# A hybrid attention, RWKV-7 and PEER block on one Trainium2 core: half of the low gate tables on ScalarE, and gate products with tokens innermost in PSUM

## The chip, the cores and the metric

The kernel runs on one core of a Trainium2 chip. The metric is the device time of one execution in microseconds (us), shown as a median over runs. The profile is one execution taken by the hardware profiler. TensorE (PE) does matmuls into PSUM, VectorE (DVE), ScalarE (ACT) and GpSimd (POOL) work on elements, and SyncE (SP) and ScalarE issue DMA transfers. TensorE has a clock of two levels, 1.2 and 2.4 GHz, of which the profile shows the granted share.

## The reference

For 512 tokens of width 1024 it computes a mixing part (sliding-window attention and an RWKV-7 recurrence, gated and projected) and a feed-forward part that picks experts by product keys (PEER). Only the second part matters here. For each token and each of 8 heads, 128 first and 128 second keys are scored; the best 16 pairs give 16 experts with softmax gates, 128 slots per token in all:

```python
s1, i1 = lax.top_k(sc[:, :, 0], PEER_TOPK)
s2, i2 = lax.top_k(sc[:, :, 1], PEER_TOPK)
...
top, pos = lax.top_k(cand, PEER_TOPK)
idx = jnp.take_along_axis(cidx, pos, axis=-1)
gate = jax.nn.softmax(top, axis=-1)
...
hpre = jnp.einsum('ckd,cd->ck', u_tab[ic], xc).astype(f32)
act = jax.nn.gelu(hpre, approximate=False) * gc
return jnp.einsum('ck,ckd->cd', act.astype(v_tab.dtype), v_tab[ic])
```

## The kernel before

For 384 of the 512 tokens the kernel doesn't gather experts; it computes all 16,384 of them densely, 128 experts (one second key, all first keys) at a time, and multiplies the activations with a dense gate that is zero where an expert wasn't picked. For the last 128 tokens the rows are gathered by indirect DMA.

The dense gate of a token is a 128 x 128 matrix over first and second keys. It is a product over the 128 slots: a one-hot table of the first key, times a one-hot table of the second key that carries the gate. To keep precision with f16 operands, the gate is scaled by GSC and split into a high part and a low part, and two products are added up in PSUM. Tokens come in 48 groups of 8. For group `i`, the function `onehots(i)` makes both one-hot tables in one VectorE comparison (L551, tile "ot", five buffers), `gated(i)` makes the high table (L557, tile "hi", four buffers) and, in place, the low table (L558, in "ot"), both on VectorE with the tokens of a pair innermost (GB2 = 2), and `gates(i)` does 16 matmuls of 128 x 128 x 128 (L571) into two PSUM tiles of 4 tokens and lets ScalarE bring each to SBUF (L574, "stg") with tokens innermost. After two groups a slice is kept on chip (L576, "gt0") and the 16 tokens' matrices go to DRAM by a DMA on ScalarE's queue (L577).

The stage around it is `window`. There the order of TensorE and of VectorE is the one written by hand: group `i` issues `onehots(i + 1)`, `gated(i)`, now and then a piece of the top-k code of a later block (PIECES), `gates(i - 2)` and 4 or 8 steps of the expert stage's first matmuls (`U`, from `u_stream`). ScalarE and POOL take the order that the framework's planner gives them. The steps of `u_stream` multiply the tokens with an expert block's weights: half of them in three f32r products of split operands (L96 to L98), half in plain f32 (L342, two instructions each). ScalarE makes the high part of these weights (L139) and POOL the low part (L140); ScalarE also applies the activation to the result (L352, out of two "mm" banks of PSUM). Twelve steps (RES) are kept back for the time after the last group, when the first gated activation is made (`v_first`: POOL L365, ScalarE L101, VectorE L102). PSUM tiles named "w" have six buffers.

`Topk.topk(b)` leaves, for each block of 128 tokens, the indices in `ids` and both parts of the gate in `gps`, in f16: the high part by ScalarE (L738), the low part by POOL (L739).

```python
for i in range(NG8):
    if i + 1 < NG8:
        onehots(i + 1)
    gated(i)
    go(PIECES.get(i, ()))
    if i >= LAG:
        gates(i - LAG)
    U(UN[i % len(UN)] + UX * (i in PIECES))
    go(POST.get(i, ()))
```

Of the kernel before, what the change touches and what calls it, by code (L numbers as in the profile page):

```python
# [10 lines left out]
F32 = mybir.dt.float32  # L11
# [5 lines left out]
AF = mybir.ActivationFunctionType  # L17
# [9 lines left out]
P = 128  # L27
# [5 lines left out]
NKEY = 128  # L33
# [18 lines left out]
NG8 = TD // 8  # L52
GSC = 2.0 ** 15
PLAIN = AHEAD - 2
GB2 = 2
# [481 lines left out]
def window(tc, ps, g_dram, u_stream, qst, tst, tk, tk0, scores, late_scores, gt0, v_first, whole):  # L537
    nc = tc.nc
    V, S, G, PE = nc.vector, nc.scalar, nc.gpsimd, nc.tensor
    ids, gps, row128 = tk.ids, tk.gps, tk.row128  # L540
    with ExitStack() as st:
        tk.sp = st.enter_context(tc.tile_pool(name="sp", bufs=1, reuse_waits="tile"))
        hot = {}
        stg = []

        def per_token(t):
            return t.rearrange("p (a b) -> p a b", b=GB2)[:, :, None, :].to_broadcast([P, t.shape[1] // GB2, NKEY, GB2])

        def onehots(i):
            hot[i] = ob.tile([P, 2, 8 // GB2, NKEY, GB2], F16, name="ot", bufs=OB + 1)  # L550
            V.tensor_tensor(hot[i].rearrange("p a q e t -> p (a q) e t"), per_token(ids[:, i]),  # L551
                            row128[:, None].to_broadcast([P, 16 // GB2, NKEY, GB2]), op=ALU.is_equal)

        def gated(i):
            ot = hot[i]
            hi = ob.tile([P, 8 // GB2, NKEY, GB2], F16, name="hi", bufs=OB)
            V.tensor_mul(hi, ot[:, 1], per_token(gps[:, i, 0:8]))  # L557
            V.tensor_mul(ot[:, 1], ot[:, 1], per_token(gps[:, i, 8:16]))  # L558
            hot[i] = ot[:, 0], (hi, ot[:, 1])

        def gates(i):
            o1, o2 = hot.pop(i)
            c, g8 = divmod(i, GCH // 8)
            if g8 == 0:
                stg[:] = [ob.tile([P, NKEY, GCH], F32, name="stg", bufs=2)]
            for q in range(2):
                pg = ps.tile([P, 4, NKEY], F32, name="w", bufs=6)
                for t in range(4):
                    for n in range(2):
                        qq, tt = divmod(q * 4 + t, GB2)  # L570
                        PE.matmul(pg[:, t], o1[:, qq, :, tt], o2[n][:, qq, :, tt], start=n == 0, stop=n == 1,  # L571
                                  skip_group_check=True)
                c0 = g8 * 8 + q * 4
                S.activation(stg[0][:, :, c0:c0 + 4].rearrange("p e t -> p t e"), pg, AF.Copy, scale=1.0 / GSC)  # L574
            if g8 == GCH // 8 - 1:
                S.activation(gt0[:, c], stg[0][:, :E2B], AF.Copy)  # L576
                nc.scalar.dma_start(g_dram[c], stg[0])  # L577

        us = u_stream()

        left = [AHEAD * KD - RES]

        def U(n):
            n = min(n, left[0])
            left[0] -= n
            for _ in range(n):
                next(us)

        with tc.manual_schedule(engines={mybir.EngineType.PE, mybir.EngineType.DVE}):
            tks = [tk0, *(tk.topk(b) for b in range(1, NB))]  # L590

            def go(todo):
                for b in todo:
                    next(tks[b], None)

            for h in range(HEADS):
                scores(1, h)
                go(SLOT[h])
            late_scores()
            whole()  # L600
            qst.close()
            ob = st.enter_context(tc.tile_pool(name="ob", bufs=2, reuse_waits="tile"))
            for n, todo in UN0:
                U(n)
                go(todo)
            onehots(0)
# [9 lines that stand above are left out]
            for i in range(NG8 - LAG, NG8):  # L616
                gates(i)
            v_first()
            for _ in us:
                pass  # L620
    tst.close()


class Topk:
    def __init__(self, tc, dump, ident, ps, tp, sc, idxU, idxV, ggate):
        self.tc, self.dump, self.ident, self.ps, self.tp, self.sc = tc, dump, ident, ps, tp, sc
        self.idxU, self.idxV, self.ggate = idxU, idxV, ggate
        V, G = tc.nc.vector, tc.nc.gpsimd
        self.sixteen = tp.tile([P, TOPK], U32, name="sixteen")
        V.memset(self.sixteen, 16)  # L630
        self.row16 = tp.tile([P, TOPK, TOPK], BF16, name="row16")
        self.row128 = tp.tile([P, NKEY, GB2], F16, name="row128")
        for t, w in ((self.row16, TOPK), (self.row128, GB2)):
            G.iota(t, pattern=[[1, t.shape[1]], [0, w]], base=0, channel_multiplier=0,
                   allow_small_or_imprecise_dtypes=True)
        self.ids = tp.tile([P, NG8, 16], F16, name="ids")
        self.gps = tp.tile([P, NG8, 16], F16, name="gps")

    def top16(self, jobs):
        V = self.tc.nc.vector  # L640
        for vals, idx, src in jobs:
            V.max(vals[:, 0:8], src)
        for vals, idx, src in jobs:
            V.max_index(idx[:, 0:8], vals[:, 0:8], src)
        for vals, idx, src in jobs:
            V.match_replace(src, vals[:, 0:8], src, FMIN)
        for vals, idx, src in jobs:
            V.max(vals[:, 8:16], src)
        for vals, idx, src in jobs:
            V.max_index(idx[:, 8:16], vals[:, 8:16], src)  # L650

    def topk(self, b):
        nc, ps, sc, ident, dump = self.tc.nc, self.ps, self.sc, self.ident, self.dump
        V, S, G, PE = nc.vector, nc.scalar, nc.gpsimd, nc.tensor
        ids, gps, tp = self.ids, self.gps, self.tp
# [18 lines left out]
        for r in range(4):  # L674
            na, w = 1 << r, TOPK >> r
# [51 lines left out]
        if b < ND:  # L727
            yield
            pt = ps.tile([P, 3, P], F32, name="w", bufs=6)
            for n, src in enumerate((i1, i2, gf)):  # L730
                PE.transpose(pt[:, n], src, ident)
            gr = slice(b * P // 8, (b + 1) * P // 8)
            g = sp.tile([P, HEADS, TOPK], F32, name="rg").rearrange("p h s -> p (h s)")
            g = g.rearrange("p (i t) -> p i t", t=8)
            for n, dst in enumerate((ids[:, gr, 0:8], ids[:, gr, 8:16], g)):
                S.activation(dst, pt[:, n].rearrange("p (i t) -> p i t", t=8), AF.Copy, scale=GSC if n == 2 else 1.0)
            hi, lo = gps[:, gr, 0:8], gps[:, gr, 8:16]
            S.activation(hi, g, AF.Copy)  # L738
            G.tensor_sub(lo, g, hi)  # L739
        else:  # L740
            V.scalar_tensor_tensor(self.idxU, i1, float(NKEY), i2, op0=ALU.mult, op1=ALU.add)
            V.scalar_tensor_tensor(self.idxV, i2, float(NKEY), i1, op0=ALU.mult, op1=ALU.add)
            V.tensor_copy(self.ggate, gf)
# [705 lines left out]
```

## Time and profile before

| what | value |
|---|---|
| time, median of 3 runs | 1825.45 us (1820.81 to 1827.6) |
| the profiled execution's own time | 1818.6 us |
| its span, first to last instruction | 1816.7 us |
| mean granted TensorE clock | 0.978 |
| stage of the gate tables | about 664 to 886 us |

In rows of the trace, times are microseconds unless marked ns. A group of instructions is written as line, engine, operation, output tile and input tiles, shapes and count, then busy time and mean ns of one, then the idle time of the engine just before them and what ended it. "PEld" is the weight load of TensorE. The end of a matmul is modelled; the pace of TensorE is read from start to start.

### The profile page before, as it was taken

The numbers are of one execution on the slowest core, as the hardware profiler recorded it, in microseconds if no ns is written. First come the engines' busy times: TensorE is split into PE (matmuls) and PEld (weight loads), VectorE is DVE, ScalarE is ACT, GpSimd is POOL, SyncE is SP. The second block draws the span as 40 slices with busy tenths as digits, with TensorE's granted clock in tenths as the row PEclk, the third lists the DMA queues.
The fourth block names the chain that finished last, engine by engine and source line by source line (L and its number), as shares of the span: only waits on it lengthen the run. The fifth ranks groups of instructions, "written<-read, shape, count | busy, mean of one in ns | idle before, by whom it ended". The sixth has DMA issues, their size and how long they took to land.

```text
span 1816.7 us, 30025 instructions
## 1 busy us (share of the span) xinstructions
PE 1714.3 (94%) x10933; PEld 1432.8 (79%) x10933; DVE 1349.0 (74%) x2564; ACT 720.4 (40%) x1415; POOL 780.5 (43%) x634
## 2 busy tenths in 40 slices
PE   7998899899999789898799999999999999998998
PEld 6765666667778668676689999999999999997886
DVE  4667665754535999999677777677788788788886
ACT  4553132221335436666633333333333333333334
POOL 5534232311155412122255555555455555556450
PEclk9998899999999889999899999999999999999999
DMA  6221111111564225563799999999989999998864
GB/s 210 81 64 41 36 42 48 36 48 54 184 205 133 88 76 178 199 216 142 243 320 325 305 313 325 317 303 317 321 302 318 322 302 320 327 309 290 297 222 167
DMA packets 193397, 378.98 MB, mean 209 GB/s; under 512 B 18624, under 2 KB 65472, under 8 KB 190176
## 3 DMA queue, kind: packets, MB, share of 16 engines
q1 hardware_dynamic: 97344, 175.71, 28.5%
q0 software_dynamic: 36864, 134.23, 22.1%
q10 hardware_dynamic: 59040, 67.12, 10.9%
q8 instruction: 86, 1.41, 0.3%
q14 instruction: 63, 0.52, 0.1%
HBM read 342.12 MB, written 33.55 MB: 207 GB/s over the span
## 4 chain that ended last, share of the span: by engine, by line
PE 45%; DVE 3%; issue 1%; DMA 1%; ACT 0%; POOL 0%; DVEq 0%; SPq 0%; POOLq 0%; ACTq 0%
PE w L96 8%; PE w L97 8%; PE w L98 8%; PE mm L96 7%; PE mm L98 7%; PE mm L97 7%; DMA vraw<-v_t 1%; DVE al L102 1%; DVE gacc L416 1%; DVE vl L102 0%; DVE wxl L102 0%; ACT w L467 0%; DVE gt L466 0%; DMA wraw<-v_t 0%; DVE wl L102 0%
## 5 line engine op out<-in xcount | busy, mean ns | idle before, releaser
L140 POOL TENSOR_TENSOR wl<-wraw,wh 128x512 fp32r<-128x512 f32 (+1 forms) x95 | 133.1, 1401 | 347.4 <-ACT wh L139 292.8
L96 PE MATMUL w<-vh,al 128*128 128x512 f32 x678 | 265.1, 391 | 6.8 <-DVE al L102 6.7
L97 PE MATMUL w<-vl,ah 128*128 128x512 f32 x678 | 264.6, 390 | 0.0
L98 PE MATMUL w<-vh,ah 128*128 128x512 f32 x678 | 264.4, 390 | 0.0
L399 POOL DMA_INDIRECT grow<-v_t,idxV x128 | 175.8, 1373 | 185.3 <-DVE gacc L416 152.1
L352 ACT ACTIVATE big<-mm 128x384 f32<-128x384 f32 x128 | 63.0, 492 | 464.6 <-PE mm L98 372.6
L399 POOL DMA_INDIRECT grow<-u_rows,idxU x128 | 167.9, 1312 | 183.4 <-DVE grow L406 164.3
L140 DVE TENSOR_TENSOR wl<-wraw,wh 128x512 fp32r<-128x512 f32 x101 | 103.8, 1028 | 153.2 <-ACT wh L139 128.4
L96 PE MATMUL mm<-x2h,wl 128*128 128x384 f32 (+1 forms) x576 | 199.2, 346 | 7.6 <-ACT big L352 6.2
L98 PE MATMUL mm<-x2h,wh 128*128 128x384 f32 (+1 forms) x576 | 191.7, 333 | 0.0
L97 PE MATMUL mm<-x2l,wh 128*128 128x384 f32 (+1 forms) x576 | 191.7, 333 | 0.0
L139 ACT ACTIVATE wh<-wraw 128x512 fp32r<-128x512 f32 (+1 forms) x196 | 122.4, 624 | 133.1 <-PE mm L763 53.0
L416 DVE SCALAR_TENSOR_TENSOR gacc<-grow,act,gacc 128x1024 f32<-128x1024 f32 x127 | 166.2, 1309 | 2.2
L102 DVE TENSOR_TENSOR vl<-vraw,vh 128x512 fp32r<-128x512 f32 x217 | 147.8, 708 | 25.5 <-ACT vh L101 25.1
L96 PEld LDWEIGHTS w<-vh,al 128*128 128x128 f32 x678 | 127.6, 188 | 33.3 <-DVE al L102 9.9
L365 POOL TENSOR_TENSOR big<-big,gt 128x384 f32<-128x384 f32 x128 | 135.8, 1064 | 34.3 <-ACT gt L576 21.2
L406 DVE SCALAR_TENSOR_TENSOR grow<-grow,xg 128x1024 f32<-128x1024 f32 x128 | 150.1, 1217 | 0.0
L98 PEld LDWEIGHTS w<-vh,ah 128*128 128x128 f32 x678 | 127.4, 188 | 26.8
L97 PEld LDWEIGHTS w<-vl,ah 128*128 128x128 f32 x678 | 127.5, 188 | 23.0
L96 PE MATMUL mm<-x2h,wxl 128*128 128x384 f32 (+1 forms) x436 | 143.5, 329 | 0.0
L97 PE MATMUL mm<-x2l,wxh 128*128 128x384 f32 (+1 forms) x436 | 143.4, 329 | 0.0
L98 PE MATMUL mm<-x2h,wxh 128*128 128x384 f32 (+1 forms) x436 | 143.4, 329 | 0.0
(388 smaller groups left out, 3944.0 us busy)
## 6 DMA issues: line engine op xcount, KB each, us to landing
wraw<-u_t SPq DMA_DIRECT2D x256, 256.0 KB
vraw<-v_t SPq DMA_DIRECT2D x217, 256.0 KB
g_dram<-stg ACTq DMA_DIRECT2D x24, 1024.0 KB
gt<-g_dram ACTq DMA_DIRECT2D x60, 384.0 KB
wraw<-wz SPq DMA_DIRECT2D x72, 256.0 KB
wraw<-v_t SPq DMA_DIRECT2D x39, 256.0 KB
wraw<-wq SPq DMA_DIRECT2D x32, 256.0 KB
wraw<-wproj SPq DMA_DIRECT2D x16, 256.0 KB
```

The lines of the kernel that those rows point to most:

```text
L96: PE.matmul(o, ll, rh, start=start, stop=False)
L97: PE.matmul(o, lh, rl, start=False, stop=False)
L98: PE.matmul(o, lh, rh, start=False, stop=stop)
L102: V.tensor_sub(lo, src, hi.bitcast(F32))
L139: S.activation(wh[:, :, :m], raw[:, :, :m], AF.Copy)
L140: lo.tensor_sub(wl[:, :, :m], raw[:, :, :m], wh[:, :, :m].bitcast(F32))
L352: S.activation(H[e], o, AF.Gelu)
L365: G.tensor_mul(ht, ht, g[:, :, e % E2B, :])
L399: G.indirect_dma_start(out=r, out_offset=None, in_=src, in_offset=bass.IndirectOffsetOnAxis(ap=idx[:, i:i + 1], axis=0))
L406: V.scalar_tensor_tensor(r, r, 1.0, xg, op0=ALU.mult, op1=ALU.mult, accum_out=hpre[:, s:s + 1])
L416: V.scalar_tensor_tensor(gacc, r, act[:, i:i + 1], gacc, op0=ALU.mult, op1=ALU.add)
```

## The change

In even groups the low table is made by ScalarE, with eight scaled copies, one for each token: each reads and writes in place the 128 elements of one token's table (every second f16 of a pair's rows) and takes that token's low gate from a new f32 tile, "gpl", as its per-partition scale. In odd groups VectorE makes it as before. "gpl" is written by one more POOL subtraction for each block. The gate products write PSUM with the four tokens innermost, so the 128 columns of a product lie 16 bytes apart, and the evacuation on ScalarE then reads PSUM in order and writes runs of four f32.

```diff
--- before.py
+++ after.py
@@ -555,7 +555,12 @@
             ot = hot[i]
             hi = ob.tile([P, 8 // GB2, NKEY, GB2], F16, name="hi", bufs=OB)
             V.tensor_mul(hi, ot[:, 1], per_token(gps[:, i, 0:8]))
-            V.tensor_mul(ot[:, 1], ot[:, 1], per_token(gps[:, i, 8:16]))
+            if i % 2:
+                V.tensor_mul(ot[:, 1], ot[:, 1], per_token(gps[:, i, 8:16]))
+            else:
+                for t in range(8):
+                    o = ot[:, 1, t // GB2, :, t % GB2]
+                    S.activation(o, o, AF.Copy, scale=tk.gpl[:, i, t:t + 1])
             hot[i] = ot[:, 0], (hi, ot[:, 1])
 
         def gates(i):
@@ -564,14 +569,14 @@
             if g8 == 0:
                 stg[:] = [ob.tile([P, NKEY, GCH], F32, name="stg", bufs=2)]
             for q in range(2):
-                pg = ps.tile([P, 4, NKEY], F32, name="w", bufs=6)
+                pg = ps.tile([P, NKEY, 4], F32, name="w", bufs=6)
                 for t in range(4):
                     for n in range(2):
                         qq, tt = divmod(q * 4 + t, GB2)
-                        PE.matmul(pg[:, t], o1[:, qq, :, tt], o2[n][:, qq, :, tt], start=n == 0, stop=n == 1,
+                        PE.matmul(pg[:, :, t], o1[:, qq, :, tt], o2[n][:, qq, :, tt], start=n == 0, stop=n == 1,
                                   skip_group_check=True)
                 c0 = g8 * 8 + q * 4
-                S.activation(stg[0][:, :, c0:c0 + 4].rearrange("p e t -> p t e"), pg, AF.Copy, scale=1.0 / GSC)
+                S.activation(stg[0][:, :, c0:c0 + 4], pg, AF.Copy, scale=1.0 / GSC)
             if g8 == GCH // 8 - 1:
                 S.activation(gt0[:, c], stg[0][:, :E2B], AF.Copy)
                 nc.scalar.dma_start(g_dram[c], stg[0])
@@ -635,6 +640,7 @@
                    allow_small_or_imprecise_dtypes=True)
         self.ids = tp.tile([P, NG8, 16], F16, name="ids")
         self.gps = tp.tile([P, NG8, 16], F16, name="gps")
+        self.gpl = tp.tile([P, NG8, 8], F32, name="gpl")
 
     def top16(self, jobs):
         V = self.tc.nc.vector
@@ -737,6 +743,7 @@
             hi, lo = gps[:, gr, 0:8], gps[:, gr, 8:16]
             S.activation(hi, g, AF.Copy)
             G.tensor_sub(lo, g, hi)
+            G.tensor_sub(self.gpl[:, gr], g, hi)
         else:
             V.scalar_tensor_tensor(self.idxU, i1, float(NKEY), i2, op0=ALU.mult, op1=ALU.add)
             V.scalar_tensor_tensor(self.idxV, i2, float(NKEY), i1, op0=ALU.mult, op1=ALU.add)
```

## Rows read from the trace of the kernel before

**Rows 1.** The page's line of busy us, share of the span and instructions of each engine.

```profile
PE 1714.3 (94%) x10933; PEld 1432.8 (79%) x10933; DVE 1349.0 (74%) x2564; ACT 720.4 (40%) x1415; POOL 780.5 (43%) x634
```

**Rows 2.** Busy time of each engine by stretch. Columns: from and to (us), length, then PE, PEld, DVE, ACT and POOL busy with their instructions, the granted TensorE clock, the DMA share and GB/s. The first stretch is the stage of the gate tables, the last lies in the expert stage.

```profile
664.00:886.00 222.00, 202.12 (x1394) 161.15 (x1393) 216.84 (x593) 141.70 (x210) 49.92 (x35) 0.95 0.52 186
679.90:748.00 68.10, 68.08 (x495) 54.19 (x492) 66.58 (x220) 43.63 (x67) 16.67 (x12) 1.00 0.56 195
837.00:869.00 32.00, 25.16 (x169) 20.51 (x168) 31.17 (x74) 19.39 (x30) 6.21 (x5) 0.89 0.41 147
869.00:886.00 17.00, 10.63 (x98) 8.79 (x99) 15.50 (x20) 12.45 (x16) 1.78 (x2) 0.70 0.68 249
1200.00:1500.00 300.00, 300.00 (x1530) 274.32 (x1529) 237.25 (x315) 109.61 (x219) 164.45 (x132) 1.00 0.92 313
```

**Rows 3.** Groups of instructions by line: first ScalarE's evacuation and VectorE's low table in the stage (660 to 895 us), then TensorE's groups from the first gate product to the last (679.9 to 885.9 us). Columns after the count: busy us, mean ns of one, idle us before them and what ended it.

```profile
L574 ACT ACTIVATE stg<-w 128x512 f32<-128x512 f32 x96 | 93.9, 1079 | 3.8 <-PE w L571 3.8
L558 DVE TENSOR_TENSOR ot<-ot,gps 128x1024 f16<-128x1024 f16 x48 | 40.0, 833 | 1.8
...
L571 PE MATMUL w<-hi,ot 128*128 128x128 f16 x384 | 54.4, 229 | 9.1 <-DVE hi L557 9.0
L571 PE MATMUL w<-ot 128*128 128x128 f16 x384 | 53.2, 228 | 4.6 <-DVE ot L558 4.6
L342 PE MATMUL mm<-wxh,wraw 128*128 128x384 f32 x108 | 44.6, 494 | 0.0
L342 PE MATMUL mm<-wxl,wraw 128*128 128x384 f32 x108 | 43.7, 486 | 0.0
L96 PE MATMUL mm<-x2h,wl 128*128 128x384 f32 x112 | 42.7, 381 | 6.2 <-ACT big L352 6.2
L97 PE MATMUL mm<-x2l,wh 128*128 128x384 f32 x112 | 39.0, 348 | 0.0
L98 PE MATMUL mm<-x2h,wh 128*128 128x384 f32 x112 | 38.9, 347 | 0.0
```

**Rows 4.** TensorE's time line, matmuls alone, at full clock (838 to 844 us) and at half clock (857 and 858 us). Columns: start, duration, engine, line, operation. The duration holds the pipeline; the pace is the distance from start to start. Between the first two lines lie 12 more gate products, between the next two five more matmuls, between the last two ten more gate products.

```profile
838.79 0.22 PE L571 MATMUL w<-hi,ot 128*128 128x128 f16 x1
...
839.54 0.22 PE L571 MATMUL w<-ot 128*128 128x128 f16 x1
...
840.18 0.33 PE L96 MATMUL mm<-x2h,wl 128*128 128x384 f32 x1
...
841.21 0.34 PE L96 MATMUL mm<-x2h,wl 128*128 128x384 f32 x1
...
842.38 0.81 PE L342 MATMUL mm<-wxl,wraw 128*128 128x384 f32 x2
...
843.02 0.81 PE L342 MATMUL mm<-wxh,wraw 128*128 128x384 f32 x2
...
857.06 0.31 PE L571 MATMUL w<-hi,ot 128*128 128x128 f16 x1
...
858.24 0.31 PE L571 MATMUL w<-ot 128*128 128x128 f16 x1
```

**Rows 5.** Who waited for whom from 660 to 920 us: us in total, times, longest.

```profile
PE w L571 <- DVE hi L557: 9.0, 2, 5.1
...
PE mm L96 <- ACT big L352: 6.2, 1, 6.2
...
PE w L571 <- DVE ot L558: 4.6, 9, 1.4
...
DVE ot L551 <- PE w L571: 0.7, 1, 0.7
```

**Rows 6.** Time line: the multiply that makes the eighth low table, and the first product of the eighth group.

```profile
700.09 0.69 DVE L558 TENSOR_TENSOR ot<-ot,gps 128x1024 f16<-128x1024 f16 x1
...
710.11 0.22 PE L571 MATMUL w<-hi,ot 128*128 128x128 f16 x1
```

**Rows 7.** VectorE's time line near the end of the stage: group 46's two multiplies and the first of group 47.

```profile
881.97 0.68 DVE L557 TENSOR_TENSOR hi<-ot,gps 128x1024 f16<-128x1024 f16 x1
882.68 0.69 DVE L558 TENSOR_TENSOR ot<-ot,gps 128x1024 f16<-128x1024 f16 x1
883.29 0.68 DVE L557 TENSOR_TENSOR hi<-ot,gps 128x1024 f16<-128x1024 f16 x1
```

**Rows 8.** ScalarE: the group of 128x128 exponentials with a per-partition operand (70 to 130 us, shapes kept apart), two neighbours in the time line of which the first is a packed evacuation, and four evacuations of gate products in a row.

```profile
L996 ACT ACTIVATE lg<-lg,nm 128x128 f32<-128x128 f32 x8 | 3.1, 389 | 3.9 <-DVE nm L990 3.9
...
111.32 0.58 ACT L1117 ACTIVATE zt<-mm 128x512 f32<-128x512 f32 x1
111.80 0.62 ACT L139 ACTIVATE wxh<-wraw 128x512 fp32r<-128x512 f32 x1
...
868.37 3.66 ACT L574 ACTIVATE stg<-w 128x512 f32<-128x512 f32 x4
```

**Rows 9.** Time line where the stage ends: the last gate product, the three evacuations that ScalarE still has, and the first matmul that needs the gated activation.

```profile
885.56 0.22 PE L571 MATMUL w<-ot 128*128 128x128 f16 x1
...
888.55 2.81 ACT L574 ACTIVATE stg<-w 128x512 f32<-128x512 f32 x3
...
894.24 0.47 PE L96 MATMUL w<-wh,wl 128*128 128x512 f32 x1 [2.15 <-DVE wl L102]
```

**Rows 10.** ScalarE's time line: copies of the top-k code behind a wait for VectorE.

```profile
747.96 2.19 ACT L669 ACTIVATE tfx<-tf 128x512 bf16<-128x512 bf16 x4 [3.82 <-DVE eq L711]
```

## The prediction, made before the changed kernel was run

> **What bounds the kernel now.** I read the page's busy times first, then the busy times by stretch, then the groups of instructions and the waits of the stretch that the change touches, and last its time line. On the page TensorE is busy for 94% of the span and VectorE for 74% [rows 1]; that mean hides two regimes. From 1200 to 1500 us, in the middle of the expert stage, TensorE is busy 300 of 300 us with the clock at 1.00 and VectorE has some 20% to spare [rows 2]: nothing of the change lies there, so that part can only slide. Between 664 and 886 us the gate tables are made, and there VectorE is busy 216.8 of 222 us and TensorE 202.1 [rows 2]. A busy TensorE need not be a full one, so I worked out what it has to do from the first gate product (679.9) to the last (885.9). Counts are in [rows 3], spacings from start to start in [rows 4]: 13 gate products in 0.75 us are 58 ns each, six split matmuls in 1.03 us 172 ns each, two plain f32 matmuls in 0.64 us 0.32 us each. 768 x 0.058 + 336 x 0.172 + 216 x 0.32 = 44.5 + 57.8 + 69.1 = 171.4. By the code as many plain steps as split ones run, two instructions each; 112 x 2 = 224, so eight records are missing: 2.6 more, 174. The stretch takes 206, so TensorE has 32 us to spare, and VectorE, over the whole stage, 5.
>
> The waits say where those 32 us are [rows 5]: TensorE waited 9.0 + 4.6 us for VectorE's tables and 6.2 us once for ScalarE; VectorE waited for TensorE 0.7 us once. The rest is the granted clock, 0.89 and 0.70 from 837 and from 869 us on, where TensorE had idled [rows 2], and steps that issue late. So VectorE's instructions, in an order written by hand, set the end of this stage, though for the first 68 us TensorE is full too (68.08 of 68.1 [rows 2]) and VectorE leads: the eighth low table starts at 700.09, its products at 710.11 [rows 6]. The lead is used up by about 837, after which TensorE waits.
>
> **The change part by part.** Removed from VectorE: the multiply of L558 for 24 of the 48 groups. In the time line L557 is followed by L558 after 0.71 us, and L558 by the next instruction after 0.61 [rows 7]. Without L558 that one follows L557 after some 0.61, so one multiply is worth 0.71, and 24 are worth 17.0 us. The other bound is the mean of one in the stage, 833 ns [rows 3], 20.0 in all; but whatever stretches some of them beyond the usual 0.69 would fall on the instruction that then runs in their place. I take 17.0.
>
> Added to ScalarE: 8 scaled copies of 128x128 in each even group, 192 in all. The nearest row is the exponential with a per-partition operand, 128x128, 389 ns [rows 8]; neighbours on ScalarE overlap by 0.10 (a 0.58 us copy is followed after 0.48 [rows 8]), so 0.29 each, 2.3 us a group, 56 us in all. A copy's source and target step by two f16, as the product's operands do; no ScalarE row shows that step, so from 0.29 (nothing for it) up to 0.41 (0.97 ns an element, the price of the evacuation's step below, on 128 elements); I take 0.29, since a step of 4 bytes is nearer to none than the evacuation's 64.
>
> Eased on ScalarE: 96 evacuations, 1079 ns each [rows 3], four in 3.66 us, so 0.87 apart [rows 8]. They now write each element 64 bytes from the last; after the change, runs of four. A packed evacuation of the same size takes 0.58 and is followed after 0.48 [rows 8]. Between 0 and 0.39 saved for each; I take the whole, since what the step costs, (1079 - 580) / 512 = 0.97 ns an element, should fall with the number of steps, 128 for 512. That is 37 us back. ScalarE's load: 141.7 of 222 [rows 2] becomes 141.7 - 37 + 56 = 160 in some 205. It stays off the path on average. With no easing it would be 198 of 205: full.
>
> Changed on TensorE: the same 768 products, but each writes 128 columns 16 bytes apart. No row of before has a stepped output. From below nothing: the gate products already step their stationary and moving operands by two elements and run at 58 / 128 = 0.45 ns a column, as the packed 384-column ones do, 172 / 384 = 0.45 [rows 4]. From above ScalarE's stepped write, 0.97 ns an element, 125 ns a product, 96 us. I take nothing, because the nearest row is TensorE's own; the 32 us spare, less the 15 that the stage shrinks by, would hide up to 17 us, 22 ns a product. The Trainium skill ("Advanced Engine Details and Errata", Memory Cachelines) speaks against it: it gives PSUM lines of 8 bytes, two f32, and says that "Any non-contiguous AP significantly slows down matmuls". It has no figure and no trace here has a stepped output; by it the sum would be that of the first rival below.
>
> Added on POOL: three more subtractions like that of L739, in a stage where POOL is busy 50 of 222 us [rows 2]; the first group's comes long before its use. Nothing.
>
> The tail. VectorE's last L558 (group 47) stays, but group 46 now waits for ScalarE: after its L557 come 2.5 us of copies and hops, and both groups' products, 16 x 0.058 = 0.9 us each, behind them: 2.5 + 1.8 = 4.3 where today it is 2.9 from that L557's end (881.97 + 0.68 [rows 7]) to the last product at 885.56 [rows 9]. Plus 1.4. Behind the products three evacuations, 2.81 us, lead to the first gated activation, for which TensorE idles 2.15 us [rows 9]; they shrink by 3 x 0.39, which takes 1.2 off that idling.
>
> A new wait: ScalarE runs in order, and 24 times a copy waits for L557. Queued behind it are the weight splits (POOL and then TensorE wait for these), the activations out of the two "mm" banks and the evacuations. One such case exists: ScalarE waited 3.82 us for VectorE's L711 [rows 10], then loaded a table, and TensorE stood 6.2 us for the activation behind it [rows 5]. As VectorE leads by some microseconds, most of the 24 will find L557 done; I allow 2 us, a third of that one case.
>
> Sum: -17.0 + 1.4 - 1.2 + 2 = -15. TensorE then has 206 - 15 = 191 us for 174 of work. The profiled execution took 1818.6, 0.4% under the median of the runs shown, 1825.45; its 1818.6 - 15 = 1803.6 corresponds to 1810 on that median.
>
> **Rivals.** *The stepped output slows TensorE* (ends slower). Where each column lands in a new place, a product may run at half rate: 107 ns, as the rows at half clock have it (11 products in 1.18 us [rows 4]), or twice its present 58. That is 768 x 0.049 = 38 to 768 x 0.058 = 44 us against 32 spare: TensorE becomes the bound and the stage 6 to 12 us longer, 1831 to 1837, and more if any of today's idling stays. It decides from 42 ns a product, 100 ns in all. For it: ScalarE's stepped write costs. Against it: TensorE's stepped reads are free. If only the accumulating half of the products pays, 19 us are added, and the stage still ends some 13 us earlier. Chance 0.30. It is the case that the Trainium skill's page named above would have.
>
> *ScalarE's order costs what VectorE saves.* Copies placed ahead of evacuations and weight splits hold them until L557, or the evacuations stay at 0.87 and ScalarE is full. Break-even is 17.0 / 24 = 0.7 us lost by TensorE for each group. For it: the 6.2 us case; against it: VectorE's lead and ScalarE's 45 idle us. 1816 to 1832. Chance 0.17.
>
> *The lead is capped.* In the first 68 us TensorE is full, and VectorE may only be as far ahead as five "ot" buffers let it; then the 8 multiplies saved there, 6 us, turn into waits of L551 for L571, and -15 becomes -9: 1813 to 1818. For it: the one wait of 0.7 us. Against it: later in the stage the wait for ScalarE that delays TensorE follows VectorE and so comes earlier too. Chance 0.13.
>
> **How the numbers follow.** The forecast (1805 to 1815) gets 0.40. Faster by over 0.5%, 9 us, about what a measurement of this kernel can tell from no change: nearly all of it, 0.38, and half of the capped lead, 0.06: 0.44. Slower: most of the stepped output, 0.22 (its lower end is within 0.5%), and some of ScalarE's order, 0.05: 0.27. The same: 0.29. The range goes from 1803 (20.0 saved, and the wait for ScalarE shorter) to 1836, near the end of the stepped output; below it 0.05 and above it 0.12 are left out. The forecast's own range is 1803 to 1816.
>
> **What would show it.** Right: 24 multiplies on L558's line, products still 58 ns apart, evacuations near 0.6 us, copies near 0.39, and the last products near 871 us. Wrong: products at 100 ns or more apart with TensorE full from 680 on; evacuations still over 1 us; TensorE waiting for ScalarE in each even group; L551 waiting for L571.

## The result, and the profile after

The changed kernel takes 1836.92 us (median of 6 runs, 1836.27 to 1839.46), the kernel before on the same chip 1822.17 (6 runs, 1818.66 to 1827.6): 1.0086 times as long, 95% interval 1.0072 to 1.01 (the two medians by themselves give 1.0081). I had forecast 1810 and a range of 1803 to 1836; the change makes the kernel 15 to 16 us slower. Of all runs below one was slow, 4294.65 us in half_layout, and the ratios leave it out.

The page's busy times of the kernel after, to be held against [rows 1]:

```profile
PE 1744.7 (95%) x10933; PEld 1464.3 (80%) x10933; DVE 1324.7 (72%) x2540; ACT 734.7 (40%) x1607; POOL 781.2 (43%) x637
```

VectorE has 24 instructions fewer and 24 us less to do, as the edit says. But TensorE, with the same number of instructions, is busy 30 us longer. Busy time by stretch, columns as in [rows 2]: the stage, ten microseconds in its middle, and its end.

```profile
664.00:886.00 222.00, 215.34 (x1251) 176.82 (x1250) 180.02 (x557) 137.49 (x351) 46.98 (x35) 0.98 0.45 162
762.00:772.00 10.00, 6.90 (x29) 6.62 (x30) 6.36 (x11) 7.13 (x18) 1.27 (x1) 0.66 0.26 106
890.00:904.20 14.20, 14.03 (x122) 13.38 (x121) 6.66 (x8) 14.17 (x42) 0.56 (x1) 1.00 0.74 270
```

In the first line VectorE fell from 216.84 to 180.02 of 222 us and TensorE rose from 202.12 to 215.34: the two have changed places. The last gate product starts at 903.87, where before it started at 885.56 [rows 9]; those 18.3 us make up the whole difference between the two profiled executions (1836.64 against 1818.6, 18.0 us). The groups of instructions from 640 to 920 us, columns as in [rows 3]:

```profile
L576 PE MATMUL w<-ot 128*128 128x128 f16 x384 | 89.3, 311 | 0.1
L576 PE MATMUL w<-hi,ot 128*128 128x128 f16 x384 | 88.1, 309 | 1.1 <-ACT stg L579 1.1
...
L551 DVE TENSOR_TENSOR ot<-ids,row 128x2048 f16<-128x2048 f16 x48 | 62.5, 1303 | 42.6 <-PE w L576 42.6
L563 ACT ACTIVATE ot<-ot,gpl 128x128 f16<-128x128 f16 x192 | 62.4, 427 | 8.8 <-DVE hi L557 8.8
...
L579 ACT ACTIVATE stg<-w 128x512 f32<-128x512 f32 x96 | 51.2, 589 | 1.5 <-PE w L576 1.4
...
L559 DVE TENSOR_TENSOR ot<-ot,gps 128x1024 f16<-128x1024 f16 x24 | 19.5, 811 | 0.9
```

The evacuations became as cheap as forecast (589 ns, from 1079) and the low tables on VectorE are 24. But a gate product takes 310 ns where it took 229, and TensorE no longer waits for VectorE's tables; VectorE waits 42.6 us for TensorE to free the "ot" buffers, where it waited 0.7 before [rows 5]. The pace is read from start to start, on TensorE's time line of the kernel after at full clock. Between the first two of these lines lie eleven more products.

```profile
700.55 0.31 PE L576 MATMUL w<-ot 128*128 128x128 f16 x1
...
701.86 0.31 PE L576 MATMUL w<-ot 128*128 128x128 f16 x1
701.92 0.42 PE L96 MATMUL mm<-x2h,wl 128*128 128x384 f32 x1
```

Twelve steps in 1.31 us are 109 ns each, against 58 ns in [rows 4]. So 768 x 0.051 = 39 us were added to a TensorE that had 32 to spare.

### The profile page after: what moved, and what is told of

Its sections match the earlier page's. It is cut to its first block, busy times and chain, and to the rows that moved or that the text cites. A ratio compares the mean times of both kernels' runs of the same rounds, so it can differ in the third digit from the quotient of the medians.

```text
span 1834.9 us, 30200 instructions
## 1 busy us (share of the span) xinstructions
PE 1744.7 (95%) x10933; PEld 1464.3 (80%) x10933; DVE 1324.7 (72%) x2540; ACT 734.7 (40%) x1607; POOL 781.2 (43%) x637
## 4 chain that ended last, share of the span: by engine, by line
PE 45%; DVE 3%; issue 1%; DMA 1%; ACT 1%; POOL 0%; DVEq 0%; POOLq 0%; ACTq 0%
PE w L97 8%; PE w L96 8%; PE w L98 8%; PE mm L96 7%; PE mm L98 7%; PE mm L97 7%; DVE al L102 1%; DVE gacc L416 1%; DMA vraw<-v_t 1%; DVE vl L102 0%; ACT w L467 0%; DVE wxl L102 0%; DVE gt L466 0%; DVE wl L102 0%; DVE gt L476 0%
## 5 line engine op out<-in xcount | busy, mean ns | idle before, releaser
L140 DVE TENSOR_TENSOR wl<-wraw,wh 128x512 fp32r<-128x512 f32 x101 | 98.8, 979 | 151.9 <-ACT wh L139 150.0
L140 POOL TENSOR_TENSOR wxl<-wraw,wxh 128x512 fp32r<-128x512 f32 (+1 forms) x60 | 88.6, 1476 | 139.0 <-ACT wxh L139 123.4
L101 ACT ACTIVATE vh<-vraw 128x512 fp32r<-128x512 f32 x217 | 129.8, 624 | 35.0 <-DMA vraw<-v_t 20.5
```

The costliest lines, as they stand in the source:

```text
L101: S.activation(hi, src, AF.Copy)
L140: lo.tensor_sub(wl[:, :, :m], raw[:, :, :m], wh[:, :, :m].bitcast(F32))
```

## The experiments

Theory A: the stepped output halves the pace of the products, and TensorE becomes the bound (A1: any step does it; A2: the cost grows with the step). Theory B: ScalarE, which takes its work in order, now holds up TensorE. Theory C: VectorE's lead is capped by the five "ot" buffers. Where the text put on record ahead of a run words a theory anew, or adds one, that wording holds for this run. In what follows "ratio" is the time over that of the kernel before, measured on the same chip, with its 95% interval; it isn't quite the quotient of the two medians.

**layout_alone: the layout without the copies.** All low tables stay on VectorE.

```diff
-                pg = ps.tile([P, 4, NKEY], F32, name="w", bufs=6)
+                pg = ps.tile([P, NKEY, 4], F32, name="w", bufs=6)
...
-                        PE.matmul(pg[:, t], ...
+                        PE.matmul(pg[:, :, t], ...
...
-                S.activation(stg[0][:, :, c0:c0 + 4].rearrange("p e t -> p t e"), pg, AF.Copy, scale=1.0 / GSC)
+                S.activation(stg[0][:, :, c0:c0 + 4], pg, AF.Copy, scale=1.0 / GSC)
```

> Kernel before with the second half of the change alone: gate products write PSUM with the tokens innermost, all low tables stay on VectorE. Theory A (the stepped output of a product sets TensorE to half its pace, 109 ns a product as in the changed kernel, and that alone makes the stage longer): 109 ns here too, evacuations near 0.58 us, TensorE full, and a time of 1832 to 1842 us, that of the changed kernel or a little above, because it is VectorE's 17 us that are missing and VectorE is not the bound. Theory B (the loss comes from ScalarE, whose copies hold up the evacuations and weight splits behind them): without copies no loss, 1815 to 1826 us, whatever the pace of the products.

Measured: 1828.1 us, ratio 1.0051 (1.0036 to 1.0067). Busy time by stretch, columns as in [rows 2]:

```profile
664.00:886.00 222.00, 221.44 (x1329) 183.60 (x1329) 213.54 (x584) 106.99 (x204) 51.20 (x35) 1.00 0.49 177
```

TensorE is full for 221.44 of 222 us at a clock of 1.00: its 32 us are used up, and the last product starts at 893.96, 8.4 us late. By the sum that is 39 - 32 = 7. The layout by itself makes the kernel slower, although it takes 35 us off ScalarE (141.70 to 106.99). So the pace of the products costs time by itself, as theory A says; but the time lies under A's 1832 to 1842 and over B's 1815 to 1826, and the changed kernel is slower still, so A isn't the whole.

**copies_alone: the copies without the layout.** The first hunk of the change and "gpl", with the PSUM tile, the products and the evacuation as before.

> Changed kernel with PSUM as before: even groups' low tables by ScalarE's copies, products write 128 neighbouring columns, evacuations write stg with a 64-byte step. Theory A: products at 58 ns, evacuations at 1.08 us, ScalarE with 37 us more to do than in the changed kernel and nearly full in the stage; VectorE's saving shows in part: 1806 to 1820 us. Theory B: ScalarE is the bound, its order delays TensorE: 1826 us or more, with TensorE waiting for ScalarE's activations and copies.

Measured: 1831.98 us, ratio 1.0067 (1.0049 to 1.0085). The products are fast again (226 ns in the row below), and still the kernel is slower. Busy time by stretch, then the group of evacuations and of products, then two lines of the waits (us in total, times, longest), all of this kernel:

```profile
664.00:886.00 222.00, 201.21 (x1329) 158.36 (x1328) 187.44 (x565) 177.80 (x374) 51.69 (x37) 0.95 0.49 173
```

```profile
L579 ACT ACTIVATE stg<-w 128x512 f32<-128x512 f32 x96 | 92.2, 1076 | 0.0
...
L576 PE MATMUL w<-hi,ot 128*128 128x128 f16 x384 | 55.1, 226 | 4.2 <-ACT stg L579 4.1
```

```profile
DVE ot L551 <- PE w L576: 32.5, 14, 5.0
PE mm L96 <- ACT big L352: 16.6, 9, 5.8
```

ScalarE is busy 177.80 us, and TensorE waits nine times, 16.6 us in all, for its activations, where it waited once and 6.2 us in [rows 5]. That is theory B, and so is the time, but in a kernel whose evacuations were not eased; the next one eases them.

**copies_stepped_read: copies, packed products, and a cheap evacuation.** As copies_alone, with the tokens gathered by ScalarE's read: it steps by 512 bytes through PSUM and writes runs of four f32.

```diff
-                S.activation(stg[0][:, :, c0:c0 + 4].rearrange("p e t -> p t e"), pg, AF.Copy, scale=1.0 / GSC)
+                S.activation(stg[0][:, :, c0:c0 + 4], pg.rearrange("p t e -> p e t"), AF.Copy, scale=1.0 / GSC)
```

> As copies_alone, but the step is moved to the reading side of the evacuation: ScalarE reads PSUM with a 512-byte step and writes runs of four f32. Theory A: products at 58 ns; if a stepped read of PSUM costs ScalarE nothing, evacuations take 0.58 us and the time is the one that was predicted for the change, 1803 to 1813 us; if it costs what the stepped write did, 1.08 us and the time of copies_alone. Theory B: 1826 us or more in either case, as the copies are there.

Measured: 1811.11 us, ratio 0.9953 (0.9936 to 0.997): faster than before, and 1.3% faster than the changed kernel (1.0086 / 0.9953), from which it differs only in which engine steps through PSUM. Groups from 640 to 920 us:

```profile
L576 PE MATMUL w<-hi,ot 128*128 128x128 f16 x384 | 51.7, 221 | 1.8 <-ACT stg L579 1.8
L579 ACT ACTIVATE stg<-w 128x512 f32<-128x512 f32 x96 | 50.8, 589 | 0.9 <-DMA g_dram<-stg 0.9
```

The stepped read is free for ScalarE, 589 ns as in the kernel after; the stepped write was not free for TensorE. ScalarE has the same copies and evacuations as in the kernel after, so B alone doesn't explain why that one is slow.

**pairs: the change with columns 8 bytes apart.** This tells A1 from A2.

```diff
-                pg = ps.tile([P, NKEY, 4], F32, name="w", bufs=6)
+                pg = ps.tile([P, 2, NKEY, 2], F32, name="w", bufs=6)
...
-                        PE.matmul(pg[:, :, t], ...
+                        PE.matmul(pg[:, t // 2, :, t % 2], ...
...
+                S.activation(stg[0][:, :, c0:c0 + 4].rearrange("p e (a t) -> p a e t", t=2), pg, AF.Copy, scale=1.0 / GSC)
```

> Changed kernel with the products writing PSUM in pairs of tokens, so that the columns of a product are 8 bytes apart instead of 16, and evacuations writing runs of two f32. If any step away from the neighbouring column costs the whole (theory A1): 109 ns a product, and the changed kernel's time within 4 us. If the cost grows with the step (theory A2): some 80 ns a product, 768 x 0.029 = 22 us less on TensorE, and 1812 to 1822 us. Evacuations between 0.58 and 1.08 us under both.

Measured: 1839.11 us, ratio 1.0101 (1.0081 to 1.012). Its groups of products are those of the kernel after to the last digit shown; its evacuations, which write runs of two f32, are nearly as cheap as those with runs of four:

```profile
L576 PE MATMUL w<-ot 128*128 128x128 f16 x384 | 89.3, 311 | 0.1
...
L579 ACT ACTIVATE stg<-w 128x512 f32<-128x512 f32 x96 | 52.3, 603 | 1.1 <-PE w L576 1.0
```

Half the step, the same price: A1 for these two steps.

**stepped_read_alone: the kernel before with only that cheaper evacuation.**

> Kernel before with only the evacuation changed: products write neighbouring columns, ScalarE reads PSUM with a 512-byte step and writes runs of four f32; all low tables on VectorE. Evacuations 0.59 us instead of 1.08 in every theory. Theory A (VectorE's instructions set the end of the stage, ScalarE's load only matters through the one 6.2 us wait and the tail): 0 to 4 us below the kernel before. Theory B (ScalarE's place in the order is what delays TensorE, so freeing 37 us of it is what gave copies_stepped_read its 9 us): 7 to 12 us below.

Measured: 1819.0 us, ratio 0.9992 (0.9975 to 1.0009). ScalarE's busy time in the stage falls from 141.70 to 102.34 us and nothing comes of it: by itself the easing of ScalarE is worth nothing, so the gain of copies_stepped_read is the copies' (VectorE's), which the dear evacuations had hidden.

**half_layout: stepped products in odd groups only**, 384 of 768, on top of stepped_read_alone.

```diff
+                pg = ps.tile([P, 4 * NKEY], F32, name="w", bufs=6)
+                pg = pg.rearrange("p (e t) -> p t e", t=4) if i % 2 else pg.rearrange("p (t e) -> p t e", t=4)
```

> As stepped_read_alone, but the products of every other group (384 of 768) write with the 16-byte step. Theory A (TensorE has 32 us to spare in this stage, and a product at 109 ns takes 51 ns of it): 20 us more of TensorE's work, all inside the 32, so the time of stepped_read_alone within 4 us, where the whole layout cost 9 us over the kernel before. Theory B (each slowed product is paid in full): half of what the whole layout costs, 4 to 6 us, on top of stepped_read_alone, with no threshold.

Measured: 1820.79 us, ratio 1.0001 (0.9985 to 1.0017). Busy time by stretch:

```profile
664.00:886.00 222.00, 213.85 (x1377) 174.31 (x1376) 217.09 (x593) 105.44 (x209) 50.93 (x35) 0.98 0.50 183
```

384 x 0.051 = 20 us more work on TensorE cost 1.6 us by the ratios (1.0001 against 0.9992 in stepped_read_alone), which isn't clear of noise, and 3.8 us by the last product of the one profiled execution of each (887.88 against 884.06); 39 cost 8 or 9 (layout_alone). So most of the 32 us that I had counted as spare were spare; whether the 20 us were hidden in full isn't shown.

**no_low_even: the saving on VectorE by itself.** The kernel before without the low tables of even groups, made by nobody: their products take the one-hot table as it is.

> Kernel before without the low tables of even groups: the multiply is left out and nothing takes its place, so half of the gates lose their low part (the one-hot table stands in for it). It prices the first term of the prediction's sum by itself. Theory A: VectorE's 17 us come off the stage nearly whole, 13 to 18 us below the kernel before. Theory C (TensorE is full in the first half of the stage, so that VectorE's lead is capped and only part shows): 6 to 11 us below, with waits of L551 for the gate products that the kernel before has not.

Measured: 1806.07 us, ratio 0.9911 (0.9885 to 0.9937), 16 us off; the last product starts at 871.16. VectorE waits for the "ot" buffers 4.2 us in all, twice, so theory C takes next to nothing here.

**copies_fourth and copies_third: fewer copies.** copies_stepped_read with every fourth (12) or third (16) low table on ScalarE, where it had 24.

```diff
-            if i % 2:
+            if i % 4:
```

> As copies_stepped_read, but ScalarE makes the low table of every fourth group only (12 of 48). Theory A (VectorE's saving pays in proportion and ScalarE has room): between stepped_read_alone and copies_stepped_read, about 4 us above the latter. Theory B (each set of copies also delays TensorE through ScalarE's order): as fast as copies_stepped_read or faster, since half of the copies are gone.

> As copies_stepped_read and copies_fourth, with ScalarE making every third low table (16 of 48). Under the reading that VectorE's saving grows by 0.7 us for each table moved and ScalarE's order takes back more the more copies there are, so that a half and a fourth came out alike (0.9953, 0.9946): 0.992 to 0.995, the best of the three or level. Under the reading that copies cost nothing on ScalarE: between the other two.

Measured: 1810.32 us, ratio 0.9946 (0.9925 to 0.9967), and 1812.88, 0.9951 (0.9932 to 0.997). Twelve tables bring 0.54%, 9.8 us, about all that twelve multiplies are worth (12 x 0.71 = 8.5); sixteen and twenty-four bring no more. The three differ by less than their intervals, so copies_third doesn't decide between its two readings. All three beat the kernel before by about as much as a measurement here can tell from no change, and the changed kernel by 1.3 to 1.4%.

**layout_no_low_even: the layout with VectorE unburdened and no copies.** layout_alone without the low tables of even groups; against the kernel after it lacks the copies and "gpl", which only they read.

> Changed kernel without ScalarE's copies: the 16-byte step for all products, VectorE makes low tables in odd groups, nobody in even ones (half of the gates lose their low part). Theory A (two costs add up in the changed kernel: TensorE full at 109 ns a product, and ScalarE's copies which hold up an activation that TensorE waits for): the second is gone here, no wait of 4 us or more for ScalarE near 765 us, and a time 5 to 9 us below the changed kernel's ratio of 1.0086, about that of layout_alone (1.0051) or somewhat under it, as the last groups no longer wait for VectorE. Theory D (the changed kernel's whole loss is TensorE's pace, and layout_alone is faster for another reason): 1.007 or more, as with the copies.

Measured: 1823.98 us, ratio 1.0018 (1.0006 to 1.0029), last product at 891.97. Busy time by stretch:

```profile
664.00:886.00 222.00, 222.00 (x1336) 184.59 (x1335) 190.53 (x564) 107.01 (x204) 52.55 (x35) 1.00 0.50 178
878.00:892.20 14.20, 14.20 (x125) 14.04 (x124) 11.23 (x13) 7.76 (x15) 1.66 (x1) 1.00 0.76 273
```

TensorE is full throughout; taking 24 multiplies off VectorE brings 0.3% where it brings 0.9% with packed products. It ends where the sum says a full TensorE must: its first product starts at 679.55, and 679.55 + 174 + 39 = 892.6. So the stepped output eats VectorE's saving and a little more. But the kernel after is slower than that by 1.0086 - 1.0018 = 0.7%, 12 us: a second cost, and it comes with the copies. It is larger than the 5 to 9 us that I expected, and theory D, by which TensorE's pace is the whole loss, is out. Where, the progress of the products shows: group 15's first starts at 754.65 here and at 754.36 in the kernel after, group 18's at 769.26 and 776.57. So 7.6 us are lost at one place. ScalarE's time line there, of the kernel after:

```profile
755.79 0.63 ACT L139 ACTIVATE wh<-wraw 128x512 fp32r<-128x512 f32 x1 [5.14 <-DMA wraw<-u_t]
756.33 2.18 ACT L563 ACTIVATE ot<-ot,gpl 128x128 f16<-128x128 f16 x7
758.52 1.28 ACT L696 ACT_TABLE_LOAD   x1
759.82 0.31 ACT L696 ACTIVATE ge<-ge 128x128 f32<-128x128 f32 x1
760.03 2.17 ACT L675 ACTIVATE tfx<-tf 128x512 bf16<-128x512 bf16 x4
762.11 1.06 ACT L579 ACTIVATE stg<-w 128x512 f32<-128x512 f32 x2
763.17 1.28 ACT L352 ACT_TABLE_LOAD   x1
764.47 0.49 ACT L352 ACTIVATE big<-mm 128x384 f32<-128x384 f32 x1
```

and TensorE's, of the same kernel; the first line is the last of a group's products:

```profile
760.30 0.31 PE L576 MATMUL w<-ot 128*128 128x128 f16 x1
765.10 0.66 PE L96 MATMUL mm<-x2h,wl 128*128 128x384 f32 x1 [4.49 <-ACT big L352]
```

ScalarE stands 5.14 us at a weight split whose DMA is late; behind it are queued seven copies, a table load, the copies of the top-k code, two evacuations, another table load, and only then the activation that frees TensorE's "mm" bank. TensorE idles 4.49 us and then works at half clock until about 771 us: its split matmuls start 0.32 us apart, where before the wait they start 0.17 apart (762 to 772 us: clock 0.66, 6.90 of 10 us busy). In layout_no_low_even the planner put the wait and the table loads in another order:

```profile
755.71 0.62 ACT L139 ACTIVATE wh<-wraw 128x512 fp32r<-128x512 f32 x1
756.23 1.06 ACT L575 ACTIVATE stg<-w 128x512 f32<-128x512 f32 x2
757.30 1.28 ACT L352 ACT_TABLE_LOAD   x1
758.59 0.49 ACT L352 ACTIVATE big<-mm 128x384 f32<-128x384 f32 x1
```

The same activation comes 5.9 us earlier and TensorE doesn't wait (10 of 10 us busy at clock 1.00 from 762 to 772). The seven copies themselves are 2.2 of these 5.9 us; the rest is the first table load and the copies of the top-k code, which here run ahead of that weight split and in the kernel after stand behind it.

The kernel before has a stall at this place, too: TensorE stands there behind copies of the top-k code that wait for VectorE [rows 10], 6.2 us [rows 5]. Its line, of the kernel before:

```profile
754.38 0.66 PE L96 MATMUL mm<-x2h,wl 128*128 128x384 f32 x1 [6.17 <-ACT big L352]
```

From group 16's first product to group 17's the kernel before takes 11.2 us, the kernel after 10.4, and the two kernels with the stepped output and no copies (layout_alone and layout_no_low_even) take 3.8. So the copies don't bring a stall that the kernel before lacked; they keep one that isn't there where only the products are slow.

The rest is lost in short waits of TensorE for ScalarE. Group 39's first product comes 8.6 us after that of layout_no_low_even (878.19 against 869.63), group 41's 11.3 (891.18 against 879.88), the last one 11.9 (903.87 against 891.97). Three lines of TensorE, of the kernel after:

```profile
878.19 0.27 PE L576 MATMUL w<-hi,ot 128*128 128x128 f16 x1 [0.93 <-ACT stg L579]
...
880.57 0.41 PE L96 MATMUL mm<-x2h,wl 128*128 128x384 f32 x1 [0.48 <-ACT big L352]
...
889.02 0.41 PE L96 MATMUL mm<-x2h,wl 128*128 128x384 f32 x1 [1.12 <-ACT big L352]
```

Besides these 2.5 us, most of group 40's products come in pairs 0.29 us apart, the pace of the copies that make its table at that moment. Only 0.6 us is lost after group 41's first product, although ScalarE is full there (14.17 of 14.20 us from 890 on, against 7.76 in the stretch of layout_no_low_even above). That ScalarE causes these losses is read from the trace; no run changed it alone.

## Why the prediction was wrong

**What bounds the kernel** was right, and so was the spare of TensorE: most of 20 us of added work was hidden (half_layout), and of 39 all but 8 or 9 (layout_alone).

**VectorE's term** was about right: 17.0 forecast, 16 measured by the ratio (no_low_even; its interval is 11 to 21) and 14.4 in the traces (last product 871.16 against 885.56). That this is the 871 I had written is luck: my figure held the tail and the 2 us for ScalarE as well. And 5.0 of the 14.4 us come at one place, the stall behind the top-k copies: group 17 starts 11.2 us after group 16 in the kernel before, 6.2 in no_low_even. The waiting for buffers that I gave a rival of its own is 4.2 us in no_low_even, where the saving shows nearly whole. The 42.6 us in the kernel after are VectorE ahead of a slower TensorE, not shown to be a cause: layout_no_low_even has 29.3 with TensorE full throughout.

**The evacuations** were right: 589 ns for a forecast 580. So were the **copies**: 427 ns for 389, and seven in 2.18 us, 0.29 apart as forecast (the last one's end taken off), with a step of four bytes. ScalarE's load was to be 160 us and is 155.7 from 664 to 904.2; its sum was right, too.

**The stepped output, taken at nothing, is the step that failed.** I chose the stepped reads of TensorE as the nearest row, 0.45 ns a column. They say nothing of its writes: a column 8 or 16 bytes from the last costs 109 / 128 = 0.85 ns. What the step adds, 51 ns a product, lies between my bounds, nothing and the 125 ns from ScalarE's stepped write, and nearer to the lower; neither row had the price. Both the product that starts a sum and the one that adds to it pay (309 and 311 ns), so the half case that I named doesn't arise. The first rival had it: 107 ns, a break-even at 100, TensorE as the bound. The Trainium skill ("Advanced Engine Details and Errata", Memory Cachelines) had spoken against my choice: lines of two f32 in PSUM, and matmuls slowed significantly by any access that isn't contiguous. The traces agree, with 58 ns against 109.

**ScalarE's order, allowed 2 us, is a term of the sum that was mis-sized.** It measures 12 us in the changed kernel (1.0086 against 1.0018) and some 8 with packed products (0.9953 against 0.9911; these two differ in the evacuation as well, which by itself was worth nothing). I had reckoned the wait of a copy for VectorE's L557, which is 8.8 us over three times in the kernel after; what cost most was something else, the copies and two table loads queued between a late weight DMA and the activation that TensorE stood waiting for (7.6 us). It is the place of the 6.2 us case of the kernel before, of which my 2 us were a third.

The first rival said that the products alone would make the stage 6 to 12 us longer. They make it 6.4 us longer in the trace (layout_no_low_even, 891.97 against 885.56) and the kernel 3 us slower by the ratio (1.0018); the rest up to the measured 15 or 16 is ScalarE's order. So the rival's mechanism makes only a part of the loss. That 1836.92 lies within its 1831 to 1837 is partly luck: these were reckoned from 1825.45, and the kernel before took 1822.17 beside the changed one.

The whole, from last product to last product in the profiled executions: -14.4 for VectorE's saving (885.56 to 871.16), +20.8 for the stepped output (to 891.97), +11.9 for the copies (to 903.87): +18.3. The shares hold for the parts put in in this order; with packed products the copies cost less.

**What stays open**: whether the 8 us that the copies cost with packed products can be had back by another order on ScalarE; no run changed that order by itself.

## What to carry to other kernels

A free stepped read on an engine says nothing of its stepped write: gather or transpose where the evacuating engine reads PSUM, and leave the matmul's output packed. Work moved to an engine with idle time isn't hidden by its mean load: on a queue kept in order, look at what stands behind its late DMAs and table loads, and count the moved instructions there. And once the spare of the next engine is known (32 us here), hold each added term against it before the saving is booked, for the saving shrinks that spare too.

## What the runs showed of the hardware

A matmul of 128 f16 columns took 58 ns with packed f32 output and 109 ns with columns 8 or 16 bytes apart, at full clock. ScalarE's evacuation of 128x512 f32 took 589 ns when it read PSUM at a step of 512 bytes and wrote runs of 16 bytes, 603 ns when it wrote runs of 8 bytes (pairs), 1079 ns when it read in order and wrote at a step of 64 bytes. Other steps and sizes weren't run.
